# First two pairs multiplied as they come, an eighth bank for two blocks, fourth products last, and other planner assumptions in a two-layer encoder kernel

## The chip, the cores and the metric

The kernel runs on one core of one Trainium2 chip. The metric is the device time of one execution in microseconds (us), the median of three runs. Before the change it is 2682.38 us (2681.67 to 2683.91).

## The reference

Two layers of an encoder on 256 tokens of width 4096, in float32. The two large products of a layer, with `w_in` (4096 x 11264) and `w_out` (4096 x 4096), are nearly all the arithmetic.

```python
for l in range(DEPTH):                                  # DEPTH = 2
    h = rmsnorm(x, norm_w[l])
    proj = h @ w_in[l]
    aq, ak, av, ag, rq, rk, rv, rg = jnp.split(proj, SPLIT_POINTS, axis=-1)
    ...
    a_out = (jax.nn.silu(ag) * gqa_attention(aq, ak, av)).astype(x.dtype)
    ...
    r_out = (jax.nn.silu(rg.astype(jnp.float32)) * r).astype(x.dtype)
    x = x + jnp.concatenate([a_out, r_out], axis=-1) @ w_out[l]
return rmsnorm(x, final_norm)
```

## The kernel before, in words

**Blocks and pairs.** The output columns of the large products are cut into 30 blocks of 1024 columns: per layer 11 of `w_in` (`BLOCKS`) and 4 of `w_out`. The 4096 rows that are summed over are cut into 16 pairs of 256. `block()` (L1225) runs through the pairs and adds up 128x512 products in banks of the accumulator memory, named M1 to M7 (the profile calls all of them M). A scheme that saves multiplications is used: each of the five pairs in `SEVEN` (0, 3, 6, 9, 12) takes 7 products, each of the other eleven 8. In the latter, two of the eight products use a difference of two quarters of the activations, a third array `x3` (profile: `x`), beside `x8h` and `x8l`.

**Parts.** A float32 number is kept as a high part and a low part that TensorE multiplies in one pass each. `product()` (L849) issues three matmuls for one product: high x high (L851), low weights x high (L852), high weights x low (L853). So a block has (5 x 7 + 11 x 8) x 3 = 369 matmuls. Weights come by SyncE's queue into `wraw` (5 buffers), ScalarE casts them to `whi`, VectorE subtracts to get `wlo` (rings of 5 pages). For a pair of `SEVEN`, VectorE first forms sums of weights, `wsum`. For five pairs (`FAR_PAIRS`) the second page's low part comes otherwise: ScalarE writes -`fhi` to `flo`, and a DMA on GpSimd's queue adds the weights to it from memory (L476). The activations are split in the same way by `split_pair()` (L516): a tile `full`, scaled by the norm's gains (`nw`), becomes `x8h`, `x8l`, `x3` or `x7h`, `x7l` by way of the sums `xf`.

**The order of the work** is written by a planner that runs when the program is built. It keeps an assumed clock of TensorE (`now.t`) and of VectorE and ScalarE (`Clock`), with costs such as `vector_cost` and `STEP_V`. After every product `tick()` (L771) asks `Weights.room()` whether one more step of other work (splits in `waiting`, steps of attention and retention in `tasks` and `lanes`) fits without making the weights late by these assumptions, and if so writes that step. At most `AT_ONCE` tasks are begun at a time. When a pair's operand is needed and not there, `need()` (L626) writes all the steps that it lacks at that place. Nothing of this runs on the chip: there, each engine goes through its fixed list and waits on semaphores.

**The two ends.** At the start (L1497 and on) 36 matmuls on zeros are issued (`warm()`), then the first rows of x and of weights are loaded, and pair 1 and pair 0 are split before their products. At the end, `last_combine()` (L1382) adds the last banks and the residual, squares, forms the norm for row half 0 after M3 and for row half 1 after M4, scales eight pieces of each half (`finish()`) and stores each by a DMA on SyncE's queue (L1438). In the last block the products of pair 15, and one product of pair 14 in M4, stand behind all others; M4's three are the very last.

Of the kernel before, what the change touches and what calls it, by code (L numbers as in the profile page):

```python
# [41 lines left out]
STEP_V, STEP_S = 1.0, 1.3  # L42
# [5 lines left out]
STORE, FETCH = 8.0, 12.0  # L48
FAR_LANDING = 11.0
MARGIN = 0.0  # L50
# [7 lines left out]
AT_ONCE = 2  # L58
# [4 lines left out]

SEVEN = (0, 3, 6, 9, 12)

# [67 lines left out]
]  # L133
EIGHTS = [_p for _p in range(NP) if _p not in SEVEN]
# [4 lines left out]
def pages_of(group, first=False):  # L139

    one = [(group[0], _k) for _k in (PAGE_A, PAGE_T, PAGE_B, PAGE_U)]
    rest = [(_p, _k) for _p in group[1:] for _k in (PAGE_A, PAGE_B)]
    order = []
    if first:
        order += rest[:2]
        rest = rest[2:]
    for _i, _v in enumerate(one):
        order += [_v] + rest[_i : _i + 1]
    return order + rest[len(one) :]
# [7 lines left out]
def slots_of(group, first=False):  # L157

    for _p, _k in pages_of(group, first):
        if _p in SEVEN:  # L160
            yield [(_b, _p, (ALL, _a), _k, _h) for _b, _a, _pg, _h in SEVEN_PRODUCTS if _pg == _k]
        else:
            yield [(_b, _p, (_i, _a), _k, _h) for _b, _i, _a, _pg, _h in EIGHT_PRODUCTS if _pg == _k]
# [5 lines left out]
BANKS = ("M1", "M2", "M3", "M4", "M5", "M6", "M7")  # L169
# [35 lines left out]
def vector_cost(name, n, kwargs):  # L205
    one = name in ("tensor_copy", "tensor_scalar", "tensor_scalar_mul", "tensor_scalar_add", "memset")
    return 0.15 + n * (0.00052 if one else 0.00104)


def scalar_cost(name, n, kwargs):  # L210
    return 0.2 + n * 0.00083 + (0.2 if kwargs.get("accum_out") is not None else 0.0)
# [3 lines left out]
def hybrid_encoder(  # L215
# [137 lines left out]
    class Weights:  # L353


        def __init__(self):
            self.pages = []
            for l in range(DEPTH):
                for w, n in ((w_in, N_IN), (w_out, N_OUT2)):
                    for b in range(n):  # L360
                        for g in GROUPS:
                            start = (l, b) == (0, 0) and w is w_in
                            for slot in slots_of(g, start and g is GROUPS[0]):
                                one = Page()
                                one.pair, one.kind, one.uses = slot[0][1], slot[0][3], len(slot)
                                one.far = is_far(g, one.pair, one.kind) and not (start and g in GROUPS[:2])
                                one.src, one.begun, one.low_at, one.next = [], False, None, []
                                if one.kind == PAGE_A:
                                    one.src.append(w[l, b, one.pair, 0])
                                if one.kind == (PAGE_A if one.pair in SEVEN else PAGE_B):  # L370
                                    one.src.append(w[l, b, one.pair, 1])
                                self.pages.append(one)
            near = [g for g in self.pages if not g.far]
# [12 lines left out]
        def load(self):  # L386
            if self.loaded < len(self.todo):
# [3 lines left out]
                step = 1 if self.loaded == 1 else 2  # L391
                for k in range(0, 2, step):
                    nc.sync.dma_start(r[:, k : k + step, :], src[:, k : k + step, :])
                self.raw.append(r)

# [4 lines left out]

        def parts(self, g, src, halves=(ALL,), then=None):

            g.hi = t(wp, [P, 2, NB], "whi", RING, F32R)
            g.lo = t(wp, [P, 2, NB], "wlo", RING, F32R)
            for h in halves:
                ac.copy(g.hi[:, h, :], src[:, h, :])
            g.high_at = ac.until + PASS

            def low():
                ve.after(g.high_at)  # L410
                for h in halves:
                    ve.tensor_sub(g.lo[:, h, :], src[:, h, :], f32(g.hi)[:, h, :])
# [6 lines left out]
        def far_parts(self, g, src):  # L419

            g.hi = t(wp, [P, 2, NB], "fhi", FAR, F32R)
            g.lo = t(wp, [P, 2, NB], "flo", FAR, F32R)
            ac.copy(g.hi, src)
            ac.activation(g.lo, f32(g.hi), AF.Copy, scale=-1.0)
            g.high_at, g.low_at = ac.until, ac.until + FAR_LANDING
            self.adds.append((ac.until, partial(nc.gpsimd.dma_start, g.lo, g.src[0], accum_op=ALU.add)))
            self.load()

        def begin(self, g):
# [4 lines left out]
            elif g.pair not in SEVEN:  # L434
                halves = (slice(0, 1), slice(1, 2)) if g is self.order[0] else (ALL,)
                self.parts(g, self.taken(), halves, self.load)
# [13 lines left out]
            elif g.kind == PAGE_B:  # L450
                self.parts(g, self.b, (slice(1, 2),), self.load)
# [46 lines left out]

    weights = Weights()
# [16 lines left out]
    def split_pair(p, v, whole, stage):  # L516

        gains = gains_of(p, stage)
        now_first = stage == 0 and p == 1
# [5 lines left out]
        if gains and not now_first:  # L525
            for i in range(2):
                u = v[:, :, i].rearrange("p m a t -> p (a m) t") if whole is None else whole[:, i]
                ac.activation(u, u, AF.Copy, scale=gains[i])
            yield
# [25 lines left out]
        else:  # L555
# [4 lines left out]
            if now_first:  # L560
                for i in range(2):
                    ac.activation(hi[:, i], whole[:, i], AF.Copy, scale=gains[i])
                yield
                for i in range(2):
                    ve.scalar_tensor_tensor(
                        lo[:, i], whole[:, i], gains[i], f32(hi)[:, i], op0=ALU.mult, op1=ALU.subtract
                    )
                yield
                ve.tensor_sub(x0, x0, x1)
                for i in range(2):  # L570
                    ac.activation(g4[0][:, i], x0[:, i], AF.Copy, scale=gains[i])
                yield
                for i in range(2):
                    ve.scalar_tensor_tensor(
                        g4[1][:, i], x0[:, i], gains[i], f32(g4[0])[:, i], op0=ALU.mult, op1=ALU.subtract
                    )
            else:
                if whole is None:
                    u = [w.rearrange("p i (m a t) -> p i m a t", m=MT, t=BLK) for w in (hi, lo)]
                    pieces = [(u[0][:, i], u[1][:, i], v[:, :, i]) for i in range(2)]  # L580
                else:
                    pieces = [(hi, lo, whole)]
                for h, _, src in pieces:
                    ac.copy(h, src)
                yield
                for h, w, src in pieces:
                    ve.tensor_sub(w, src, f32(h))
# [10 lines left out]
        yield  # L598

# [171 lines left out]
    def tick():  # L771
# [5 lines left out]
        while True:  # L777
# [3 lines left out]
            for v in waiting[:SPLITS] + (lanes + running() if room else []):  # L781
# [5 lines left out]
            waiting[:] = [v for v in waiting if not v.done]  # L787
            clear()
# [436 lines left out]
    def block(after_pair, phase, then, first_order=False, order=LAST_ORDER, last=None):  # L1225
# [7 lines left out]
        for g in GROUPS:  # L1233
            for slot in slots_of(g, first_order and g is GROUPS[0]):
                flat += slot
        if first_order:

            flat[:4] = sorted(flat[:4], key=lambda v: (v[4], v[2][1] == 2))

        used = list(dict.fromkeys((v[1], v[3]) for v in flat if not is_far(None, v[1], v[3])))[-RING:]  # L1240
# [7 lines left out]
        first = {b: next(i for i, v in enumerate(flat) if v[0] == b) for b in BANKS}  # L1248
        final = {b: max(i for i, v in enumerate(flat) if v[0] == b) for b in BANKS}
        left = {}  # L1250
# [5 lines left out]
        for n, (bank, p, index, k, h) in enumerate(flat):  # L1256
            tight[0] = n < 3 or n >= len(flat) - 7
            if p in firsts:
                firsts.remove(p)
                need(p, phase)  # L1260
                now.wait(operand_at[p])
# [4 lines left out]
            if n == first[bank]:  # L1266
                acc[bank] = t(pm, [P, NB], bank)
            if p in SEVEN:
# [7 lines left out]
            product(acc[bank], a, at((g.hi, g.lo), ALL, h), n == first[bank], n == final[bank])  # L1276
            follow()
            if n == final[bank]:
                finished.append((bank, partial(last or combine, bank, acc, c)))
                if bank == order[0] or n == len(flat) - 1:  # L1280
                    follow(True)
            g.uses -= 1
            if not g.uses:
                using.remove(g)
                for one in g.next:
# [11 lines left out]
    def combine(bank, acc, c):  # L1297
# [9 lines left out]
        elif bank == "M5":  # L1307
# [74 lines left out]
    def last_combine(res):  # L1382
# [10 lines left out]
        def last(bank, acc, c):  # L1393
# [17 lines left out]
            elif bank == "M3":  # L1411
# [61 lines left out]
    def first_rows(c):  # L1473
        full[c] = page([P, KG * SEQ], "full")
        step = KG * SEQ // (2 if c == 0 else 1)
        for k in reversed(range(0, KG * SEQ, step)):
            nc.sync.dma_start(full[c][:, k : k + step], xT[c, :, k : k + step])

# [7 lines left out]
    def made(p):  # L1486

        one = next(v for v in waiting if v.pair == p)
        while not one.done:
            one.step()  # L1490
        waiting.remove(one)

    def begun():
        weights.begin(next(g for g in weights.order if not g.begun))
        weights.low_parts(True)

    warm()  # L1497
    first_rows(0)
    weights.load()
    turn = Turn(0, first_rows)  # L1500
# [3 lines left out]
    for _ in range(2):  # L1504
        waiting[1].step()
    begun()
    made(1)
    weights.load()
    first_rows(1)
    for _ in range(RAWS - 2):  # L1510
        weights.load()
    first_rows(2)
    begun()
    made(0)
    begun()
    split_operand(1, 0)
    made(2)
    begun()
    made(3)
    begun()  # L1520


    for l, L in enumerate(layers):
        for bi, (one, _) in enumerate(BLOCKS):
# [9 lines left out]
            c = block(after, 2 * l + 1, 2 * l + 1 + (bi == N_IN - 1), start)  # L1534
# [81 lines left out]
```

## Time and profile before

| | |
|---|---|
| median of three runs | 2682.38 us |
| the profiled execution's own time | 2678.84 us |
| its span, first to last instruction | 2676.8 us |
| TensorE (PE) matmuls busy | 2620.1 us, 98% |
| VectorE (DVE) busy | 2134.8 us, 80% |
| ScalarE (ACT) busy | 1799.5 us, 67% |
| granted TensorE clock, mean | 0.991 |
| DMA, mean | 255 GB/s |

The helper that records VectorE's and ScalarE's operations has one line, L200, so these are told apart by their tiles. A profile row names the engine, the line, the operation, out<-in and the count. "PEq", "SPq" and the like are the engines' issuing queues. Idle time of an engine that nobody waits for costs nothing.

### The profile page before, as it was taken

Reading aid. Unit: us, or ns where it says so; the run is one execution under the profiler, and the core shown is the slowest. Engines: PE = TensorE matmul, PEld = TensorE weight load, DVE = VectorE, ACT = ScalarE, POOL = GpSimd, SP = SyncE. Lnnn points to the kernel's source line nnn. Section 1 sums busy time; section 2 is a strip of 40 time slices with the busy share of each in tenths; the row PEclk is TensorE's granted clock in tenths of the full one; section 3 lists DMA queues with packets and bytes.
Section 4 is the critical chain, followed back from the end, with each engine's and each line's share of the span. In section 5 each row is a group of like instructions: output and inputs, shape, how many; then the busy total and the mean of one; then the engine's idle time right before and its main releaser. Section 6 shows DMA issues by size and latency. Waiting matters only on the chain.

```text
span 2676.8 us, 33938 instructions
## 1 busy us (share of the span) xinstructions
PE 2620.1 (98%) x11778; PEld 2169.8 (81%) x11778; DVE 2134.8 (80%) x2620; ACT 1799.5 (67%) x2554; POOL 366.2 (14%) x508
## 2 busy tenths in 40 slices
PE   8999999999999999999999999999999999999997
PEld 6877888888888878888787888887888888788886
DVE  7787878879868888777887878877887688886775
ACT  7766776766665678655876666775676567786554
POOL 0011211211111010111111111211210111010000
PEclk8999999999999999999999999999999999999999
DMA  7888889888778777988887888887887787778886
GB/s 252 284 259 283 251 265 290 281 255 275 229 235 252 239 239 221 287 278 254 284 257 229 271 278 275 264 273 241 266 255 222 238 261 238 226 235 263 252 268 192
DMA packets 200828, 683.90 MB, mean 255 GB/s; under 512 B 24144, under 2 KB 30800, under 8 KB 200656
## 3 DMA queue, kind: packets, MB, share of 16 engines
q1 hardware_dynamic: 147760, 521.27, 55.8%
q0 software_dynamic: 52896, 160.46, 25.9%
q8 instruction: 92, 1.51, 0.2%
q14 instruction: 80, 0.66, 0.1%
HBM read 637.60 MB, written 44.04 MB: 255 GB/s over the span
## 4 chain that ended last, share of the span: by engine, by line
PE 82%; DVE 8%; DMA 6%; ACT 2%; issue 2%; POOL 1%; SPq 0%; DVEq 0%; ACTq 0%; POOLq 0%
PE M L852 26%; PE M L853 26%; PE M L851 26%; DVE wlo L200 4%; DMA wraw<-in_w_in 3%; DMA flo<-in_w_in 2%; DVE wsum L200 1%; PE ps L852 1%; PE ps L853 1%; PE ps L851 1%; DMA wraw<-in_w_out 1%; ACT whi L200 1%; DVE cb L200 0%; DVE ca L200 0%; DMA flo<-in_w_out 0%
## 5 line engine op out<-in xcount | busy, mean ns | idle before, releaser
L200 DVE TENSOR_TENSOR wlo<-wraw,whi 128x1024 fp32r<-128x1024 f32 (+1 forms) x813 | 895.5, 1119 | 305.3 <-ACT whi L200 300.4
L200 ACT CAST whi<-wraw 128x1024 fp32r<-128x1024 f32 (+1 forms) x813 | 779.7, 969 | 509.0 <-PE M L853 365.6
L851 PE MATMUL M<-whi,x8h 128*128 128x512 f32 x1536 | 600.8, 391 | 1.1 <-ACT whi L200 0.6
L852 PE MATMUL M<-wlo,x8h 128*128 128x512 f32 x1536 | 600.2, 391 | 1.2 <-DVE wlo L200 1.2
L853 PE MATMUL M<-whi,x8l 128*128 128x512 f32 x1536 | 599.1, 390 | 0.0
L851 PE MATMUL M<-whi,x7h 128*128 128x512 f32 x1050 | 410.1, 391 | 6.8 <-DVE cb L200 6.8
L852 PE MATMUL M<-wlo,x7h 128*128 128x512 f32 x1050 | 409.5, 390 | 1.7 <-DVE wlo L200 1.7
L853 PE MATMUL M<-whi,x7l 128*128 128x512 f32 x1050 | 409.1, 390 | 0.0
L200 DVE TENSOR_TENSOR wlo<-wsum,whi 128x1024 fp32r<-128x1024 f32 x300 | 365.3, 1218 | 25.9 <-ACT whi L200 25.7
L200 ACT CAST whi<-wsum 128x1024 fp32r<-128x1024 f32 x300 | 314.8, 1049 | 97.8 <-PE M L853 92.5
L851 PEld LDWEIGHTS M<-whi,x8h 128*128 128x128 f32 x1536 | 289.9, 189 | 61.8 <-ACT whi L200 1.7
L852 PEld LDWEIGHTS M<-wlo,x8h 128*128 128x128 f32 x1536 | 289.9, 189 | 61.2 <-DVE wlo L200 2.2
L853 PEld LDWEIGHTS M<-whi,x8l 128*128 128x128 f32 x1536 | 289.7, 189 | 60.6
L200 ACT CAST fhi<-wraw 128x1024 fp32r<-128x1024 f32 x148 | 155.7, 1052 | 199.2 <-PE M L853 191.8
L476 POOL DMA_DIRECT2D flo<-in_w_in x108 | 97.1, 899 | 1100.2 <-ACT flo L200 1008.0
L851 PEld LDWEIGHTS M<-whi,x7h 128*128 128x128 f32 x1050 | 197.6, 188 | 49.3 <-DVE cb L200 8.4
L852 PEld LDWEIGHTS M<-wlo,x7h 128*128 128x128 f32 x1050 | 197.6, 188 | 42.3 <-DVE wlo L200 2.3
L853 PEld LDWEIGHTS M<-whi,x7l 128*128 128x128 f32 x1050 | 197.5, 188 | 41.1
L200 DVE TENSOR_TENSOR wsum<-wraw 128x1024 f32<-128x1024 f32 x150 | 182.8, 1219 | 48.2 <-DMA wraw<-in_w_in 37.1
L851 PE MATMUL M<-whi,x 128*128 128x512 f32 x512 | 200.9, 392 | 11.8 <-ACT x L200 10.8
L852 PE MATMUL M<-wlo,x 128*128 128x512 f32 x512 | 200.9, 392 | 1.9 <-DVE wlo L200 1.9
L853 PE MATMUL M<-whi,x 128*128 128x512 f32 x512 | 201.0, 393 | 0.7 <-DVE x L200 0.7
(223 smaller groups left out, 3401.5 us busy)
## 6 DMA issues: line engine op xcount, KB each, us to landing
wraw<-in_w_in SPq DMA_DIRECT2D x703, 512.0 KB, 5.0
wraw<-in_w_out SPq DMA_DIRECT2D x256, 512.0 KB, 4.8
flo<-in_w_in POOLq DMA_DIRECT2D x108, 512.0 KB, 7.8
flo<-in_w_out POOLq DMA_DIRECT2D x40, 512.0 KB, 7.4
full<-next_dram POOLq DMA_DIRECT2D x18, 512.0 KB, 8.4
p_dram<-room POOLq DMA_DIRECT2D x64, 128.0 KB, 4.9
pT<-p_dram POOLq DMA_DIRECT2D x16, 512.0 KB, 8.7
next_dram<-room POOLq DMA_DIRECT2D x40, 128.0 KB, 5.4
```

The costliest lines, as they stand in the source:

```text
L200: return call(out, *args, **kwargs)
L476: self.adds.pop(0)[1]()
L851: nc.tensor.matmul(out, a[0], b[0], start=start, stop=False)
L852: nc.tensor.matmul(out, a[0], b[1], start=False, stop=False)
L853: nc.tensor.matmul(out, a[1], b[0], start=False, stop=stop)
```

## The change

It has five parts.

1. **Pairs 1 and 0 of the first block are multiplied as they come** (`NATIVE`). Their weights are loaded into `fhi`, `flo` and `wsum` buffers that stand empty at that time (`load_whole`), their activations are only scaled, and one float32 matmul (L1379) stands for each product in place of three. Pair 0 takes 8 products there, as the third array isn't formed. Both pairs are still split afterwards, for the blocks that follow.
2. **In the first two blocks an eighth bank stands in for the third array** (`PLAIN`, `PLAIN_PRODUCTS`). M8 uses the bank `ps` that attention and retention use later. `x3` is formed afterwards from the parts (`third()`), a step at a time, before the third block.
3. **In the last block the M4 products of five pairs** (`DELAYED`) stand behind all others: 10 products, 30 matmuls, in place of 3 products, 9 matmuls. The weights that they need are written to rooms of activations that are no longer used (`dead_room`), so those pages are split in halves.
4. **The last scalings are dealt out otherwise**: all eight pieces of row half 0 directly behind its norm.
5. **Other planner assumptions**: `STEP_V`, `S_FIXED`, `MARGIN`, `AT_ONCE`.

```diff
-STEP_V, STEP_S = 1.0, 1.3
+STEP_V = 1.6
+STEP_S = 1.3
+V_FIXED = 0.15
+S_FIXED = 0.12
-MARGIN = 0.0
+MARGIN = 0.2
-AT_ONCE = 2
+AT_ONCE = 3
+DELAYED = (10, 11, 13, 14, 15)
+NATIVE = (1, 0)
+WHOLE = 4
+PLAIN = 2
...
+PLAIN_PRODUCTS = [
+    ("M3", 1, 0, PAGE_A, 1),
+    ("M8", 1, 1, PAGE_A, 1),
...
+        def load_whole(self, n):
+            g = self.wholes[n]
+            tag, bufs, dt = (("fhi", FAR, F32R), ("flo", FAR, F32R), ("wsum", 2, F32), ("wsum", 2, F32))[n]
+            g.raw = f32(t(wp, [P, 2, NB], tag, bufs, dt))
+            for k in (1, 0) if n == 0 else (ALL,):
+                nc.sync.dma_start(g.raw[:, k, :], g.src[0][:, k, :])
+            g.begun, g.high_at, g.low_at = True, 0.0, 0.0
...
+    def third(p, hi, lo, g, one):
+        while held[0] + pledged() >= PAGES:
+            yield
+        one.at_work = True
+        v = page([P, 2, 2, P], "x3f")
+        d, e = v[:, 0], v[:, 1]
+        for u, v in ((d, hi), (e, lo)):
+            ve.tensor_sub(u, f32(v)[:, :, :P], f32(v)[:, :, P:])
+        ve.tensor_add(d, d, e)
+        yield
+        ac.copy(g[:, 0], d)
+        yield
+        ve.tensor_sub(g[:, 1], d, f32(g)[:, 0])
...
-            return v[1] == NP - 1 or (last and v[0] == order[-1] and v[1] == NP - 2 and (v[1], v[3]) in used)
+            return v[1] == NP - 1 or last and v[0] == order[-1] and v[1] in DELAYED
...
+                if first_order and p in NATIVE:
+                    while p not in as_it_comes:
+                        next(v for v in waiting if v.pair == p).step()
+                    now.wait(as_it_comes[p][1])
+                else:
+                    need(p, phase)
+                    while not plain and any(v.pair == p for v in thirds):
+                        third_step()
...
+            if g.whole:
+                nc.tensor.matmul(acc[name], a, g.raw[:, h, :], start=n == first[name], stop=n == final[name])
+                now.t += WHOLE * MM[NB]
+            else:
+                product(acc[name], a, (g.hi[h], g.lo[h]), n == first[name], n == final[name])
...
+        elif bank == "M8":
+            ve.tensor_add(cb[:, 1, :], cb[:, 1, :], acc["M8"])
+            free_bank()
...
                 r[0] = last_rstd(0)
-                for n in (0, 2):
-                    finish(0, n, ac)
+                for n, e in ((0, ac), (1, ve), (2, ac), (3, ve), (5, ve), (4, ac), (6, ve), (7, ve)):
+                    finish(0, n, e)
             elif bank == "M4":
                 combine(bank, acc, c)
                 square(1, c, 0)
-                finish(0, 7, ve)
                 r[1] = last_rstd(1)
-                for n, e in ((1, ve), (6, ve), (3, ve), (4, ac), (5, ve)):
-                    finish(0, n, e)
...
     warm()
     first_rows(0)
+    weights.load_whole(1)
+    first_rows(1)
     weights.load()
+    for n in range(2, 2 * len(NATIVE)):
+        weights.load_whole(n)
+        weights.load()
...
-            c = block(after, 2 * l + 1, 2 * l + 1 + (bi == N_IN - 1), start)
+            c = block(after, 2 * l + 1, 2 * l + 1 + (bi == N_IN - 1), start, plain=l == 0 and bi < PLAIN)
```

How the instructions move is shown at three places, before and after, in the order in which they stand on one engine.

TensorE, the first products of the program, right behind the 36 matmuls on zeros. Before (`whi`, `wlo` are parts of weights, `x8h`, `x8l` parts of pair 1's activations, the numbered M are banks):

```order
L851 MATMUL M_248<-whi,x8h 128x512
L852 MATMUL M_248<-wlo,x8h 128x512
L853 MATMUL M_248<-whi,x8l 128x512
L851 MATMUL M_258<-whi,x8h 128x512
L852 MATMUL M_258<-wlo,x8h 128x512
L853 MATMUL M_258<-whi,x8l 128x512
```

Now (`fhi`, `flo`, `wsum` hold whole weights here, `full` is the scaled x):

```order
L1379 MATMUL M_195<-fhi,full 128x512
L1379 MATMUL ps<-fhi,full 128x512
L1379 MATMUL M_207<-fhi,full 128x512
L1379 MATMUL M_209<-fhi,full 128x512
L1379 MATMUL M_207<-flo,full 128x512
L1379 MATMUL ps<-flo,full 128x512
L1379 MATMUL M_195<-flo,full 128x512
L1379 MATMUL M_209<-flo,full 128x512
L1379 MATMUL M_195<-wsum,full 128x512
```

Sixteen such matmuls have taken the place of 45, and nothing of ScalarE's casts or VectorE's subtractions of weights stands ahead of them: in all PE has 29 fewer.

ScalarE, in the first block of the second layer, where the last two pairs' activations (from `cb`, the end of the first layer) are scaled and cast. Before:

```order
L200 COPY ca<-M_11784 128x512
L200 CAST whi<-wraw 128x1024
L200 CAST whi<-wsum 128x1024
L200 CAST whi<-wraw 128x1024 x3
L200 ACTIVATE cb<-cb,nw 128x8x32 x4
L200 CAST x8h<-cb 128x256 x4
L200 CAST x_12422<-cb 128x256
```

Now:

```order
L230 CAST whi<-wraw 128x1024
L230 CAST whi<-wraw 128x512
L230 ACTIVATE cb<-cb,nw 128x8x32 x4
L230 CAST x8h<-cb 128x256 x4
L230 CAST fhi<-wraw 128x1024
L230 ACTIVATE flo<-fhi 128x1024
L230 CAST x_12314<-cb 128x256
L230 COPY ca<-M_11761 128x512
```

The scaling and the casts of `x8h` have moved ahead of the bank's copy to `ca`, of a far page (`fhi`, `flo`) and of five casts of weights that stood ahead of them.

ScalarE, in the sixth block of the second layer, where a far page is made and the queries `q` of the next attention group are cast. Before:

```order
L200 CAST fhi_16073<-wraw_15947 128x1024
L200 ACTIVATE flo_16074<-fhi_16073 128x1024
L200 CAST whi_16090<-wraw_16002 128x1024
L200 CAST whi_16109<-wsum_16008 128x1024
L200 CAST whi_16120<-wraw_16011 128x1024
L200 CAST whi_16137<-wraw_16045 128x1024
L200 CAST whi_16148<-wsum_16118 128x1024
L200 CAST whi_16167<-wraw_16077 128x1024
L200 CAST whi_16179<-wraw_16033 128x512
L200 CAST aqh_16185<-q_16085 128x4x128 x2
```

Now:

```order
L230 CAST fhi_16053<-wraw_15948 128x1024
L230 ACTIVATE flo_16054<-fhi_16053 128x1024
L230 CAST aqh_16059<-q_15960 128x4x128 x2
L230 CAST whi_16069<-wraw_16002 128x1024
L230 CAST whi_16090<-wsum_15999 128x1024
```

The queries' cast stands directly behind the far page in place of seven casts later; on GpSimd's queue the load of `q` is still the row ahead of that page's DMA.

More of the change, by code (lines that the diff above doesn't have):

```diff
@@ L434, in begin @@
             elif g.pair not in SEVEN:
-                halves = (slice(0, 1), slice(1, 2)) if g is self.order[0] else (ALL,)
-                self.parts(g, self.taken(), halves, self.load)
+                self.parts(g, self.taken(), then=self.load)
             elif g.kind == PAGE_A:
@@ L497, in room, with dead_room @@
             )
+    rooms = []
+    def dead_room():
+        if not rooms:
+            two = [("x3", NP - len(SEVEN), [P, 2, 2, P], "p k s t -> p (k s t)")] * 2
+            two += [(v, NP - len(SEVEN), [P, 2, SEQ], "p k s -> p (k s)") for v in ("x8h", "x8l")]
+            one = [(v, len(SEVEN), [P, 7, P], "p k t -> p (k t)") for v in ("x7l", "x7h")]
+            for n in range(16):
+                rooms.extend(two)
+                rooms.extend(one if n % 2 else ())
+        tag, bufs, shape, flat = rooms.pop(0)
+        return t(ap, shape, tag, bufs, F32R).rearrange(flat)[:, :NB]
     weights = Weights()
@@ L528, in split_pair @@
                 ac.activation(u, u, AF.Copy, scale=gains[i])
+            if stage == 0 and p in NATIVE:
+                as_it_comes[p] = (whole, ac.until + PASS)
             yield
@@ L780, in tick @@
                 return
-            for v in waiting[:SPLITS] + (lanes + running() if room else []):
+            for v in waiting[:SPLITS] + (lanes + running() + (thirds[:1] if not waiting and not (turning and turning[0].first) else []) if room else []):
                 if v.ready <= now.t:
@@ L787, in tick @@
             waiting[:] = [v for v in waiting if not v.done]
+            thirds[:] = [v for v in thirds if not v.done]
             clear()
@@ L1503, in hybrid_encoder @@
     split_operand(0, 0)
[L1504 to L1515, printed above, removed]
+    for p in NATIVE:
+        made(p, False)
+    for p in NATIVE:
+        made(p)
     split_operand(1, 0)
[L1517 to L1520, printed above, removed]
+    waiting.sort(key=lambda v: v.pair in NATIVE)
+    for _ in range(START):
+        begun()
     for l, L in enumerate(layers):
```

217 lines of the change are left out of this document (132 added, 85 removed).

## The prediction

> **What bounds the kernel now.** I read the page's head first, then the busy time by stage, to find where TensorE (PE) stands still, and then the rows of the stages where it does. The head:
>
> ```profile
> span 2676.8 us, 33938 instructions
> PE 2620.1 (98%) x11778; PEld 2169.8 (81%) x11778; DVE 2134.8 (80%) x2620; ACT 1799.5 (67%) x2554; POOL 366.2 (14%) x508
> ```
>
> PE is the bound: busy for all but 57 us. So an edit is worth what it takes from PE's work or from those gaps. The stages, PE alone (length, busy time and matmuls, granted clock, DMA share, GB/s):
>
> ```profile
> core 0: us, PE busy (x), PEclk, DMA share, GB/s
> 0.00:44.67 44.67, 32.12 (x120) 0.85 0.74 257
> 111.60:330.00 218.40, 213.10 (x951) 1.00 0.87 269
> 980.00:1000.00 20.00, 15.83 (x66) 0.93 0.68 207
> 1290.00:1310.00 20.00, 17.61 (x71) 0.91 0.87 294
> 1410.00:1425.00 15.00, 10.01 (x34) 0.77 0.55 170
> 1425.00:1840.00 415.00, 414.88 (x1896) 1.00 0.86 268
> 1840.00:1862.00 22.00, 15.54 (x63) 0.84 0.73 254
> 2300.00:2330.00 30.00, 26.33 (x114) 0.94 0.75 217
> ```
>
> From 1425 to 1840 us PE never waits. The time is lost at the two ends and in a few gaps, each followed by some microseconds at a lower clock. The start, PE's rows, then ScalarE's (ACT) first two on data:
>
> ```profile
> 1.09 5.42 PE L1484 MATMUL ps<-junk 128*128 128x256 bf16 x36 [1.09 <-DVE junk L200]
> 20.59 0.55 PE L851 MATMUL M<-whi,x 128*128 128x512 f32 x1 [1.01 <-ACT whi L200]
> 23.29 0.63 PE L852 MATMUL M<-wlo,x8h 128*128 128x512 f32 x1
> 23.72 0.63 PE L853 MATMUL M<-whi,x8l 128*128 128x512 f32 x1
> 51.09 0.39 PE L851 MATMUL M<-whi,x8h 128*128 128x512 f32 x1
> 57.89 0.39 PE L851 MATMUL M<-whi,x7h 128*128 128x512 f32 x1
> ```
>
> ```profile
> 4.32 0.91 ACT L200 ACTIVATE x8h<-full,nw 128x256 fp32r<-128x256 f32 x2 [2.07 <-DMA full<-in_xT]
> 6.49 0.62 ACT L200 CAST whi<-wraw 128x512 fp32r<-128x512 f32 x1 [1.26 <-DMA wraw<-in_w_in]
> ```
>
> From 51.09 to 57.89 lie 30 matmuls, so one takes 0.2267 us of PE. By 44.67 us, 120 - 36 = 84 real ones have run, worth 84 x 0.2267 = 19.0 us: 25.6 us are lost. VectorE (DVE) sets that pace (columns PE, PEld, DVE, ACT, POOL, then clock and DMA):
>
> ```profile
> core 0: us, PE busy (x) PEld busy (x) DVE busy (x) ACT busy (x) POOL busy (x), PEclk, DMA share, GB/s
> 0.00:20.00 20.00, 14.63 (x66) 9.33 (x66) 10.44 (x21) 10.61 (x20) 0.20 (x4) 1.00 0.72 265
> 20.00:45.00 25.00, 17.82 (x55) 13.16 (x56) 23.08 (x37) 21.73 (x38) 1.01 (x1) 0.73 0.76 253
> ```
>
> In 20 to 45 us DVE is busy for 23.1 of 25: PE waits for parts that DVE and ACT can't make faster.
>
> **The start.** Three rows price the pieces: the weight load of one matmul, a DVE step on a page of weights (whole and half pages mixed), and one on a quarter of a pair's activations.
>
> ```profile
> L851 PEld LDWEIGHTS M<-whi,x8h 128*128 128x128 f32 x1536 | 289.9, 189 | 61.8 <-ACT whi L200 1.7
> L200 DVE TENSOR_TENSOR wlo<-wraw,whi 128x1024 fp32r<-128x1024 f32 (+1 forms) x813 | 895.5, 1119 | 305.3 <-ACT whi L200 300.4
> L200 DVE TENSOR_TENSOR x<-full,x 128x256 fp32r<-128x256 f32 x34 | 13.8, 414 | 3.7 <-ACT x L200 3.7
> ```
>
> The change puts 16 whole float32 matmuls in the place of 45. The trace has none of that kind. At least one should cost what the three parts cost together, 3 x 0.2267 = 0.68 us; at most four passes with no weight load hidden, 4 x (0.2267 + 0.189) = 1.66. I take 0.907, four passes of 0.2267, as the change's own planner counts (`WHOLE`), near the row with loads hidden: 16 x 0.907 = 14.5 us. The Trainium skill (FP8 and Floating Point Precision, TensorE Precision Notes) says that true float32 makes four passes through the array; by that the sum is as taken, an estimate that no run here shows yet.
>
> The first needs a scaled quarter of x (4.32 + 0.91 = 5.2 us) and 256 KB of weights, which came by 6.49 us and now stand one place earlier in SyncE's queue; the zeros end at 6.5. So PE begins at 6.6 us and runs to 21.1. Meanwhile DVE gets ahead: of the 33.5 us that it works in the first 45 it loses the weights of pairs 0 and 1, some 8 steps x 1.12 = 9 us, and over the block the third arrays, 2 steps x 0.41 x 11 pairs = 9 us. Those come back as four steps a pair, 18 us, spread over the first two blocks, where DVE's idle fifth (80% busy over the span) covers them; they are due only in the third block, and uncovered they would cost up to 18. The eighth bank costs two more DVE additions and no PE time. To get as far as 84 matmuls had come, 39 of the three-part kind (8.8 us) follow. For waits left in the first block I take 2.5 us, between 0 (DVE stays ahead) and 8 (it is as late as in 20 to 45 us again). 6.6 + 14.5 + 8.8 + 2.5 = 32.4, against 44.67: **-12.2 us** (-18 to +6 by the bounds).
>
> **The middle.** Two gaps have their cause in the order, and the order has changed there. At the second layer's first block:
>
> ```profile
> 1415.10 1.70 ACT L200 ACTIVATE cb<-cb,nw 128x256 f32<-128x256 f32 x4
> 1416.70 1.31 ACT L200 CAST x8h<-cb 128x256 fp32r<-128x256 f32 x4
> 1418.83 0.80 PE L851 MATMUL M<-whi,x 128*128 128x512 f32 x1 [4.99 <-ACT x L200]
> ```
>
> The last two pairs' split was written only when PE needed it, behind five casts of weights; 34 matmuls (7.7 us) ran in that stage of 15, so 7.3 us are lost. Now it stands ahead of those casts: I take 1 us as left, **-6.3**. The second, in the second layer's sixth block:
>
> ```profile
> 1836.68 0.55 POOL L814 DMA_DIRECT2D q<-q_dram  x1
> 1837.20 0.94 POOL L476 DMA_DIRECT2D flo<-in_w_in  x1
> 1853.11 0.80 PE L852 MATMUL M<-flo,x8h 128*128 128x512 f32 x1 [6.46 <-DMA flo<-in_w_in]
> ```
>
> The far page's DMA was issued right behind the loads of `kv` and `q`, and landed 15.9 us later. The stage lost 22 - 63 x 0.2267 = 7.7 us. In the new order `q` is cast directly behind `flo`, so the loads must have been planned for an earlier time: I take 0.7 as left, **-7.0**. If `q` is not there, ACT stands still behind that cast, with `whi` casts queued behind it, and the gap stays.
>
> The other gaps (5.3 us in 111 to 330, 5.0 in 980 to 1000, 3.9 in 1290 to 1310, 3.7 in 2300 to 2330) I leave as they are: what DVE and ACT have to do there is the same. `AT_ONCE`, `STEP_V` and `MARGIN` move nearly every step, so I add one new wait of the size of 1290 to 1310's, 20 - 71 x 0.2267 = **+4** (-18, if all the others go, to +17, if as much comes as I let go).
>
> **The end.**
>
> ```profile
> 2659.42 0.69 DVE L200 TENSOR_TENSOR cb<-cb,M 128x512 f32<-128x512 f32 x1 [0.67 <-PE M L853]
> 2661.46 0.69 DVE L200 TENSOR_TENSOR ca<-ca,M 128x512 f32<-128x512 f32 x1 [0.15 <-PE M L853]
> ```
>
> ```profile
> 2662.00 1.33 ACT L200 ACTIVATE ca<-ca,last 128x512 f32<-128x512 f32 x2 [1.07 <-POOL last L347]
> 2663.24 0.58 ACT L200 ACTIVATE ps<-ca 128x512 f32<-128x512 f32 x1
> 2665.17 1.95 ACT L200 ACTIVATE ca<-ca,last 128x512 f32<-128x512 f32 x3 [0.61 <-POOL last L347]
> ```
>
> ```profile
> 2662.74 0.95 SPq L1438 DMA_DIRECT2D out<-ca  x2
> 2672.11 0.59 SPq L1438 DMA_DIRECT2D out<-cb  x1
> ```
>
> Sixteen stores leave SyncE between 2662.74 and 2672.70, 0.62 us each. Row half 0's norm is ready 2.6 us after M3's addition (2659.42 to 2662.00). PE ends at 2661.4, where M4's addition begins. M3 now ends 30 matmuls, 6.8 us, ahead of that, so half 0's eight stores run from -3.5 to +1.5 us of that end, beneath M4's matmuls. Half 1's last square waited 1.1 us (2662.15 to 2663.24) behind two scalings of half 0; that goes, so its norm is there at 2664.1 in place of 2665.17, its first store 0.7 later and eight stores after 5.0: 2669.8 against 2672.70, **-2.9 us**. The halved pages make ACT and DVE's list longer by some ten half steps (0.62 us for ACT's at 6.49); ACT's idle third hides them, and uncovered they would cost 6 us.
>
> **The sum.** 2678.84 (the profiled execution, span 2676.8 and 2.0 around it) - 12.2 - 6.3 - 7.0 + 4 - 2.9 = 2654.4. The median of the runs was 3.5 us above the profiled one: 2657.9, so 2658.
>
> **Rivals.**
> - *The planner's part gives nothing.* The two gaps move to other places. For it: nearly all steps move, by assumed costs. Against it: the stages at 1410 and 1840 lose time to an order that is gone. Start and end alone: 2682.4 - 12.2 - 2.9 = 2667. Chance 0.23.
> - *The whole matmuls run at double price,* because PE waits for their weights and the clock falls. At 20.59 PE had waited 1.01 us, and behind that a matmul takes 0.43 us (23.29 to 23.72) in place of 0.2267. 16 x 0.907 more: 2672. Chance 0.10. The Trainium skill (TensorE: Matmul & The Clock Gate, What's actually happening) lets the clock fall after an idle window of about 3.4 us; the wait at 20.59 was shorter, so here the trace is the stricter.
> - *Slower: far pages come late at eight places.* In eight blocks the new order has the far page's DMA behind four `p_dram` stores on GpSimd's queue (L809), which wait for DVE's `room`.
>
> ```profile
> 1583.57 2.23 POOL L809 DMA_DIRECT2D p_dram<-room  x4 [15.60 <-DVE room L200]
> flo<-in_w_in POOLq DMA_DIRECT2D x108, 512.0 KB, 7.8
> ```
>
>  With 3.9 us lost at each, as in 1290 to 1310, it adds 31 us: 2689. It decides once the stores hold the DMA so long that less than its 7.8 us is left before PE needs the page. Against it: at 1583.57 such stores stood ahead of a far page, and PE waited nowhere from 1425 to 1840. Chance 0.07.
> - *More gaps go than I counted:* all four that I left, and no new one: 2658 - 17.9 - 4 = 2636. Chance 0.10.
>
> That the whole matmuls aren't there is excluded by PE's order, which has 29 fewer instructions.
>
> **How the numbers follow.** Forecast 0.50, rivals as given. 0.2% (5.4 us) is about what a measurement of this kernel can tell from no change: faster means below 2677. The forecast, the first two rivals and the last are there, less a little for their spread: 0.87; same 0.06; slower 0.07. The range takes in both nearer rivals and half of the way to the last: 2640 to 2673.
>
> **What would show it.** The first L1379 matmul at 6.6 us and sixteen in 14.5 us; clock 1.0 up to 45 us and the first block's end 12 us earlier; no wait for `x` near 1400 us nor for `flo` near 1835; eight stores before PE's end plus 2 us, and 12.5 us from PE's end to the last landing. It is wrong if the whole matmuls take over 1.4 us, or if PE's waits between 45 and 2640 us come to 45 us or more.

## The result and the profile after

The changed kernel takes 2642.38 us, median of four runs (2637.64 to 2644.54), against 2683.14 (2681.67 to 2684.54, four runs of the kernel before beside them): ratio 0.9846, 95% interval 0.9829 to 0.9863. That is 40.8 us less, where the forecast of 2658 made it 25; the time is inside the range.

The head of the page after:

```profile
span 2641.8 us, 33949 instructions
PE 2611.1 (99%) x11765; PEld 2162.7 (82%) x11765; DVE 2134.4 (81%) x2640; ACT 1794.0 (68%) x2559; POOL 365.7 (14%) x510
```

VectorE (DVE) and ScalarE (ACT) do as much as before. What went are waits of TensorE (PE). The largest, first before, then after (what was waited for, us in all, times, longest):

```profile
PE M L852 <- DMA flo<-in_w_in: 12.4, 6, 6.5
PE M L851 <- ACT x L200: 10.8, 3, 5.5
PE M L851 <- DVE cb L200: 6.8, 3, 3.3
```

```profile
PE M L945 <- DVE cb L230: 10.1, 4, 3.4
PE M L946 <- DMA flo<-in_w_out: 2.5, 3, 1.1
PE M L946 <- DVE wlo L230: 2.3, 2, 1.7
PE M L946 <- DMA flo<-in_w_in: 2.0, 4, 0.9
```

The waits for `x` are gone and those for `flo` and `wlo` are small; those for `cb`, an addition that frees a bank, have grown. PE's start:

```profile
1.09 6.32 PE L1598 MATMUL ps<-junk 128*128 128x256 bf16 x36 [1.09 <-DVE junk L230]
7.25 1.02 PE L1379 MATMUL M<-fhi,full 128*128 128x512 f32 x2
8.11 1.02 PE L1379 MATMUL ps<-fhi,full 128*128 128x512 f32 x2
19.27 1.88 PE L1379 MATMUL M<-wsum,full 128*128 128x512 f32 x4
20.58 0.79 PE L945 MATMUL M<-whi,x8h 128*128 128x512 f32 x1
```

A whole matmul shows as two records; from 7.25 to 8.11 runs one, so it takes 0.86 us, and sixteen take 13.7, without a wait. No wait of PE follows until 87 us.

The accounting below takes, in each trace, the time from one matmul's start to the next, less 0.2267 us (0.118 for one of 256 columns, 0.859 for a whole one), and adds up what is left over by blocks of 1024 columns, block 0 first. A block is counted from its second product on, so the wait for bank M3, which comes ahead of that product, stands with the block before. It is the time that PE loses, slow clock included; the four runs that tell most are beside the two kernels.

| us lost in blocks | before | after | e1 | e5 | e9 | e11 |
|---|---|---|---|---|---|---|
| 0 | 20.2 | 4.0 | 2.9 | 3.7 | 3.0 | 3.3 |
| 1 to 3 | 6.9 | 8.6 | 9.8 | 6.8 | 7.0 | 6.3 |
| 10, 11 | 7.1 | 4.4 | 13.5 | 6.2 | 4.7 | 4.0 |
| 14 | 4.4 | 3.1 | 6.2 | 7.2 | 1.8 | 3.6 |
| 15 (second layer's first) | 8.6 | 2.9 | 8.3 | 9.2 | 1.9 | 2.1 |
| 20 | 9.3 | 0.2 | 4.5 | 8.8 | 0.7 | 0.7 |
| 25, 26 | 6.5 | 3.2 | 13.6 | 5.4 | 3.9 | 3.2 |
| all | 65.6 | 30.5 | 63.4 | 54.3 | 27.0 | 25.5 |

The tail of the changed kernel: the additions of M3 and of M4 on DVE, the latter at PE's end, then the first and the last store of each row half on SyncE.

```profile
2623.23 0.69 DVE L230 TENSOR_TENSOR cb<-cb,M 128x512 f32<-128x512 f32 x1 [0.67 <-PE M L947]
2630.03 0.69 DVE L230 TENSOR_TENSOR ca<-ca,M 128x512 f32<-128x512 f32 x1 [1.61 <-PE M L947]
```

```profile
2626.56 0.34 SPq L1550 DMA_DIRECT2D out<-ca  x1
2630.42 0.60 SPq L1550 DMA_DIRECT2D out<-cb  x1
2633.33 0.33 SPq L1550 DMA_DIRECT2D out<-ca  x1
2637.21 0.57 SPq L1550 DMA_DIRECT2D out<-cb  x1
```

Half 0's stores run from -3.5 to +1.0 us of PE's end, and the span ends 11.8 us behind that end, against 15.3 (2661.46 to 2676.8) before.

### The profile page after: what moved, and what is told of

The parts are those of the page before. It is cut to its first block, busy times and chain, and to the rows that moved or that the text cites. A ratio compares the mean times of both kernels' runs of the same rounds, so it can differ in the third digit from the quotient of the medians.

```text
span 2641.8 us, 33949 instructions
## 1 busy us (share of the span) xinstructions
PE 2611.1 (99%) x11765; PEld 2162.7 (82%) x11765; DVE 2134.4 (81%) x2640; ACT 1794.0 (68%) x2559; POOL 365.7 (14%) x510
## 4 chain that ended last, share of the span: by engine, by line
PE 85%; DMA 5%; DVE 4%; ACT 3%; issue 2%; POOL 0%; SPq 0%; DVEq 0%; POOLq 0%; ACTq 0%
PE M L946 27%; PE M L945 27%; PE M L947 27%; DVE wlo L230 2%; DMA flo<-in_w_out 1%; DMA wraw<-in_w_in 1%; PE ps L946 1%; PE ps L947 1%; PE ps L945 1%; DMA wraw<-in_w_out 1%; DMA flo<-in_w_in 1%; ACT whi L230 1%; ACT ca L230 1%; DVE wsum L230 1%; DVE cb L230 0%
## 5 line engine op out<-in xcount | busy, mean ns | idle before, releaser
L945 PE MATMUL M<-whi,x8h 128*128 128x512 f32 x1514 | 591.8, 391 | 0.9 <-DVE ca L230 0.9
L946 PE MATMUL M<-wlo,x8h 128*128 128x512 f32 x1514 | 591.1, 390 | 0.0
L947 PE MATMUL M<-whi,x8l 128*128 128x512 f32 x1514 | 590.6, 390 | 0.0
L230 ACT CAST fhi<-wraw 128x1024 fp32r<-128x1024 f32 (+1 forms) x148 | 154.7, 1046 | 175.3 <-PE M L947 172.7
L945 PEld LDWEIGHTS M<-whi,x7h 128*128 128x128 f32 x1043 | 196.0, 188 | 51.4 <-DVE cb L230 11.8
L947 PEld LDWEIGHTS M<-whi,x7l 128*128 128x128 f32 x1043 | 196.0, 188 | 40.8
L946 PE MATMUL M<-wlo,x 128*128 128x512 f32 x476 | 186.3, 391 | 2.3 <-DVE wlo L230 2.3
L945 PE MATMUL M<-whi,x 128*128 128x512 f32 x476 | 185.9, 391 | 0.0
L947 PE MATMUL M<-whi,x 128*128 128x512 f32 x476 | 185.9, 391 | 0.0
```

What stands on the lines that cost most here:

```text
L230: return call(out, *args, **kwargs)
L945: nc.tensor.matmul(out, a[0], b[0], start=start, stop=False)
L946: nc.tensor.matmul(out, a[0], b[1], start=False, stop=False)
L947: nc.tensor.matmul(out, a[1], b[0], start=False, stop=stop)
```

## The experiments

Twelve kernels. The question was first which part had made the unexpected share of the gain, then whether that part follows a rule.

**e1, one constant put back.**

```diff
-S_FIXED = 0.12
+S_FIXED = 0.2
```

> The changed kernel with one constant put back: S_FIXED 0.2 in place of 0.12. Theory A: this constant alone makes the middle's gain (35.0 us of span, less 12.6 at the start and 3.6 behind PE's end: 18.9), because the two waits belong to the order that it sets. Then the waits for x near 1406 us (5 us) and for flo near 1843 us (6.5 us) are back, the start and the end stay as in the changed kernel, and the time is 2642.4 + 19 = 2661 (2655 to 2667). Theory B: the waits went because the first blocks were written anew and everything behind them shifted. Then the time stays at 2642 (2637 to 2648) and neither wait is there. Theory C, several constants together: half of it, about 2652.

Measured 2682.5 us (2675.6 to 2685.0), ratio to before 1.0005 (0.9993 to 1.0018): with this one constant the whole gain of the change is gone, though block 0 still loses 17 us less. More came back than any of the theories had: besides the two old waits (the one for `flo` in block 20 now 2.4 us in place of 6.5) there were two that neither kernel had, in blocks 11 and 26. One of them, on PE, and the split on ScalarE that it waited for:

```profile
1064.89 0.50 PE L945 MATMUL M<-whi,x 128*128 128x512 f32 x1 [0.80 <-ACT x L230]
1070.04 0.80 PE L947 MATMUL M<-whi,x 128*128 128x512 f32 x1 [4.42 <-DVE x L230]
```

```profile
1057.75 1.29 ACT L230 ACTIVATE ca<-ca,nw 128x256 f32<-128x256 f32 x3
1066.28 0.41 ACT L230 CAST x<-ca 128x256 fp32r<-128x256 f32 x1 [0.49 <-DVE ca L230]
```

It is the kind of block 15 before: the last pairs' split stands too late. From the scaling of the activations (1057.75) to the cast of their third array (1066.28) there are 8.5 us.

**e2, the constant alone in the kernel before.**

```diff
-    return 0.2 + n * 0.00083 + (0.2 if ...)
+    return 0.12 + n * 0.00083 + (0.2 if ...)
```

> The kernel before with one constant changed: S_FIXED 0.12 in place of 0.2, nothing else. Theory A (this constant makes the middle's gain): no wait for x near 1434 us, none for flo near 1853 us, start and end as before; 2683.1 - 19 = 2664 (2656 to 2670). Theory B (the rewritten first blocks did it): 2683 within 4 us, and waits of 5 us and more somewhere in the middle.

2664.8 (2661.9 to 2671.1), ratio 0.9949 (0.9930 to 0.9969): as theory A had it. PE loses 49.5 us in place of 65.6; block 15 loses 1.7 and block 20 0.2. A new wait for `flo` of 2.9 us came in block 4, where 6.0 us are lost.

**e5, all four assumptions put back** (`STEP_V` 1.0, `S_FIXED` 0.2, `MARGIN` 0, `AT_ONCE` 2).

> The changed kernel with all four assumptions put back (STEP_V 1.0, S_FIXED 0.2, MARGIN 0, AT_ONCE 2), so the start, the eighth bank and the end alone. S_FIXED alone put back gave 2682.5, with two waits of 5.4 us for x at 1065 and 2393 us that neither kernel had. Theory A: these two come from S_FIXED 0.2 together with STEP_V 1.6 or AT_ONCE 3, that is from assumptions that don't fit each other, and go with the old set; the waits near 1419 us (5 us) and 1848 us stay: 2682.5 - 15 = 2667 (2660 to 2673), the prediction's rival without the planner's part. Rival: the old set gives waits of the same sum at other places, 2682.

2665.7 (2658.0 to 2670.4), ratio 0.9947 (0.9927 to 0.9968). The two waits of e1 are gone; the old ones are back. ScalarE in block 15, and what PE waited there:

```profile
1395.33 1.65 ACT L230 COPY cb<-room 32x256 f32<-32x256 f32 x4
1399.52 1.05 ACT L230 CAST whi<-wraw 128x1024 fp32r<-128x1024 f32 x1
1400.47 1.05 ACT L230 CAST whi<-wsum 128x1024 fp32r<-128x1024 f32 x1
1405.89 1.70 ACT L230 ACTIVATE cb<-cb,nw 128x256 f32<-128x256 f32 x4
```

```profile
1410.19 0.79 PE L945 MATMUL M<-whi,x 128*128 128x512 f32 x1 [5.55 <-ACT x L230]
```

A cast lasts 1.05 us, but the next starts 0.95 us behind it. The planner counts 0.2 + 1024 x 0.00083 = 1.05 with the old constant and 0.97 with the new one. The split needs the activations in `cb`, which come by four sets of four copies (`COPY cb<-room`), and the planner writes a set only when its own ScalarE is nearly done with the one ahead. With the higher cost all this is written later: the last set stands 62.5 us behind the block's start (1332.8) here and 55.6 behind it (1326.7) in the changed kernel. The same rows there:

```profile
1382.29 1.65 ACT L230 COPY cb<-room 32x256 f32<-32x256 f32 x4
1389.33 1.70 ACT L230 ACTIVATE cb<-cb,nw 128x256 f32<-128x256 f32 x4
1390.93 1.31 ACT L230 CAST x8h<-cb 128x256 fp32r<-128x256 f32 x4
```

The split does not follow the copies at once. The planner begins it only when some pair of the block is finished (`turn_over()`), or when PE is to use it (`need()`). In the changed kernel it comes 62.6 us behind the block's start, and PE waits nowhere for it; in e5 it comes at 73.1. The planner's own clock, printed as it writes the two kernels, says why: in e5 the last set is done 0.7 us behind the end of pair 11, and no other pair ends before the need; in the changed kernel it is done 7.5 us ahead of the end of pair 9. Its test `room()` holds the split back in neither: it finds room after every product in between.

So the new constant does not win by being true. It fits the casts of weights, but a set of copies takes 1.65 us in both kernels, as the old constant counts it (4 x (0.2 + 256 x 0.00083)), and the new one counts 1.33. What it does is to bring the copies ahead of an earlier end of a pair.

**e9, only `S_FIXED` new**, the other three old.

> The changed kernel with the other three assumptions put back (STEP_V 1.0, MARGIN 0, AT_ONCE 2), S_FIXED left at 0.12: the fourth corner of a square whose others are 2642.4 (all new), 2682.5 (S_FIXED alone old) and 2665.7 (all old). Theory A: S_FIXED decides nearly all, the other three move little (180 of 11787 rows on TensorE stand elsewhere), so 2642 to 2648. Theory B: the other three are worth 17 us here too, one way or the other, because each order is a draw: 2652 or more.

2641.4 (2640.0 to 2645.8), ratio 0.9859 (0.9844 to 0.9873). The square is complete:

| us | other three old | other three new |
|---|---|---|
| `S_FIXED` 0.2 | 2665.7 (e5) | 2682.5 (e1) |
| `S_FIXED` 0.12 | 2641.4 (e9) | 2642.4 (changed) |

With 0.12 the other three do nothing that can be measured; with 0.2 they cost 17. The planner's part of the change is `S_FIXED`, worth 24 us (ratios to before 0.9947 and 0.9859; the kernel before took 2681 to 2683 us beside each corner).

**e6 and e7, `S_FIXED` 0.09 and 0.15.**

> The changed kernel with S_FIXED 0.09 in place of 0.12. In the trace casts of 128x1024 that follow each other start 0.95 to 0.96 us apart; 0.12 + 1024 x 0.00083 = 0.97, with 0.09 it is 0.94. Theory A (what counts is that the planner's ScalarE isn't late by its own clock): 0.09 is as near as 0.12, no wait above 3 us comes, 2642 within 5. Theory B (0.12 is one lucky order among many): waits of 4 us and more come at new places, 2650 to 2670.

> The changed kernel with S_FIXED 0.15: a cast of 128x1024 counts 1.0 us, 0.04 more than the 0.96 between two starts in the trace, half of the error that 0.2 makes. Theory A (the error decides): between 2642 and 2682, near 2655, as the order has some splits later. Theory B (each order is a lottery): anywhere from 2642 to 2682, with no relation to the error; below 2647 or above 2670 speaks for it.

2654.9 (2654.2 to 2656.3) and 2656.0 (2653.7 to 2658.5). Neither theory holds alone. With 0.09 no wait is longer than 2.2 us, but there are eight for `flo` from `w_in` (10.9 us in all); with 0.15 the split in block 15 is late again (waits of 1.2 and 3.1 us), beside 10.6 us for such `flo`. The split begins 62.2 us behind the block's start with 0.09, 62.6 with 0.12, 66.4 with 0.15 and 73.1 with 0.2, and PE waits 0, 0, 4.3 and 5.6 us for it (the last in e5): by steps, since it can begin only at the end of a pair, and not in proportion to the error. The waits for `flo`, some 10 us, fall as the order happens to be. Whether 0.12 is best because it is nearest to the casts' spacing or by its draw of short waits stays open.

**e8, the same correction for VectorE.**

```diff
-V_FIXED = 0.15
+V_FIXED = 0.07
```

> The changed kernel with V_FIXED 0.07 in place of 0.15. VectorE's subtractions of 128x1024 that follow each other start 1.14 us apart in the trace; the planner counts 0.15 + 1024 x 0.00104 = 1.215, with 0.07 it is 1.135. If costs that fit the trace are what helps, this does for VectorE what S_FIXED 0.12 did for ScalarE: of the 26 us still lost between the products some 5 to 10 go, 2633 to 2638. Rival: VectorE's surplus of 0.08 us was a reserve for waits that the planner doesn't see; without it parts come late, 2648 or more.

2661.3 (2658.3 to 2664.2), ratio 0.9931 (0.9904 to 0.9957): 19 us slower than the changed kernel, in the rival's range. Its longest waits:

```profile
PE M L946 <- DMA flo<-in_w_in: 8.4, 6, 2.8
PE M L946 <- DMA flo<-in_w_out: 6.3, 3, 3.0
PE M L946 <- DVE wlo L230: 4.6, 6, 1.0
```

The rival's reason holds only in part: the waits for `wlo`, which DVE makes, come to 4.6 us, and those for `flo`, which ACT and a DMA make, to 14.7. A cost that fits the spacing in the trace is not better by that alone.

**e3, one whole pair only** (`NATIVE = (1,)`).

> The changed kernel with NATIVE = (1,): only pair 1 is multiplied whole, eight matmuls of 0.86 us; pair 0 is split and multiplied by 7 products of three parts. Theory A: the whole matmuls pay because VectorE and ScalarE get 13.7 us ahead while they run; with half of that PE waits for parts of pair 0 or 2 behind the eighth whole matmul, at 14.1 us, for 4 to 8 us in all, less 2.1 us of work saved (8 x 0.86 = 6.9 against 21 x 0.2267 = 4.8): 2645 to 2649. Rival: pair 1 alone covers the parts (VectorE was not the limit of the start): the 2.1 us are won, 2640.

2653.4 (2651.7 to 2653.9), 11 us slower than the changed kernel, more than theory A had. Block 0 loses 12.6 us in place of 4.0:

```profile
15.32 0.50 PE L945 MATMUL M<-whi,x7h 128*128 128x512 f32 x1 [0.83 <-ACT x7h L230]
51.00 0.80 PE L947 MATMUL M<-whi,x7l 128*128 128x512 f32 x1 [3.97 <-DVE x7l L230]
```

The first four waits are the expected ones, at pair 0. The longest comes at 51 us for another pair's split; that DVE still lacks then what it lacked at 15 us fits this, but was not tested. Of the 11 us, 6.7 are there by block 1 (105.8 against 99.1); blocks 3 to 6 lose 9.7 more than in the changed kernel, in small waits, and blocks 1 and 2 lose 5.9 less.

**e4, the eighth bank in one block** (`PLAIN = 1`).

> The changed kernel with PLAIN = 1: the eighth bank stands in for the third array in the first block only. Theory A: the wait of 3.4 us for cb at 187.4 us comes from the second block's eighth bank; it goes, but the third arrays of eleven pairs (four VectorE steps of 0.41 us each, 18 us) must be made in the first block or as the second needs them, where VectorE has 10 to 17 us free: PE waits 3 to 8 us for x in the second block. Sum between -0.5 and +5: 2642 to 2647. Rival: VectorE covers the third arrays, and only the wait for cb goes: 2639.

2644.8 (2643.1 to 2645.1). The wait for `cb` at 187.4 went, and block 1 got one for `flo` and one for a third array instead:

```profile
131.67 0.50 PE L946 MATMUL M<-flo,x8h 128*128 128x512 f32 x1 [2.72 <-DMA flo<-in_w_in]
185.70 0.80 PE L947 MATMUL M<-whi,x 128*128 128x512 f32 x1 [3.87 <-DVE x L230]
```

**e11, M3's products ahead of M8's.**

```diff
-PLAIN_ORDER = ("M8", "M3", "M4", "M2")
+PLAIN_ORDER = ("M3", "M8", "M4", "M2")
```

> The changed kernel with the last products of the first two blocks in the order M3, M8, M4, M2 in place of M8, M3, M4, M2. TensorE waits 2.6 us at 99.1 and 3.4 us at 187.4 for the addition that frees M3; in VectorE's list M8's addition (0.60 us to the next start) stands ahead of M3's, and now behind it. Theory A: VectorE is behind there, so each wait becomes 0.6 us shorter, no more, and the time 1.2 us less, 2641. Theory B: the wait hangs on the order of the banks alone; with M3's last product six matmuls earlier both waits nearly go, 2637.

DVE's additions in the changed kernel, and the matmul that waits for M3's (the second `cb<-cb` below):

```profile
97.42 0.42 DVE L230 TENSOR_TENSOR x<-x3f,x 128x256 fp32r<-128x256 f32 x1
97.75 0.68 DVE L230 TENSOR_TENSOR cb<-cb,ps 128x512 f32<-128x512 f32 x1
98.35 0.68 DVE L230 TENSOR_TENSOR cb<-cb,M 128x512 f32<-128x512 f32 x1
```

```profile
99.08 0.50 PE L945 MATMUL M<-whi,x7h 128*128 128x512 f32 x1 [2.60 <-DVE cb L230]
```

In e11 they are

```profile
98.28 0.50 PE L945 MATMUL M<-whi,x7h 128*128 128x512 f32 x1 [2.04 <-DVE cb L230]
185.99 0.50 PE L945 MATMUL M<-whi,x7h 128*128 128x512 f32 x1 [0.62 <-DVE cb L230]
190.12 0.50 PE L945 MATMUL M<-whi,x8h 128*128 128x512 f32 x1 [0.76 <-DVE ca L230]
```

The first wait shrank by 0.6 us, as theory A says: weights and a step of a third array stand ahead of the additions, and DVE is behind. The second fell from 3.4 to 0.6, with a new one of 0.8 behind it, but the order made only 0.6 us of that too: PE had lost 2.6 us to a far page at 129.5, where the changed kernel loses 0.5, and so came later to the same addition. The time is 2639.6 (2636.7 to 2641.4); against 2642.4 (2637.6 to 2644.5) this is not told apart.

**e10, two pairs delayed in place of five** (`DELAYED = (14, 15)`).

> The changed kernel with DELAYED = (14, 15): M4 of two pairs, four products, 12 matmuls (2.7 us), stands behind M3's end instead of 30 (6.8 us). In the changed kernel the first store of row half 0 leaves 3.3 us behind M3's addition, and eight stores take 4.5 us; half 1 is ready 3.3 us behind TensorE's end, and the span ends 11.8 us behind it. Theory: with two pairs half 0's stores run from 0.6 to 5.1 us behind TensorE's end and half 1's wait for them until 9.5: 13.5 us from TensorE's end to the end of the span, and 1.7 us more, 2644. Rival: what helped at the end is the new dealing of the scalings, not the delayed products: 11.8 us as now, 2642.

2643.3 (2639.8 to 2645.9) is not told apart from the changed kernel either; the trace shows the end 2.9 us longer. PE's last matmul starts at 2629.02 there (2629.61 in the changed kernel), and the span ends at 2644.1. DVE tells why:

```profile
2629.31 1.28 DVE L230 TENSOR_SCALAR cb<-cb,last 128x512 f32<-128x512 f32 x3 [0.69 <-POOL last L377]
2630.50 0.75 DVE L230 SCALAR_TENSOR_TENSOR ca<-ca,last,fn 128x512 f32<-128x512 f32 x1
2631.16 0.75 DVE L230 SCALAR_TENSOR_TENSOR cb<-cb,last,fn 128x512 f32<-128x512 f32 x1
2631.82 0.68 DVE L230 TENSOR_TENSOR ca<-ca,M 128x512 f32<-128x512 f32 x1
```

Not the stores' queue is what the delay clears, as expected, but DVE: with 2.7 us between the banks M4's addition stands behind half 0's scalings. That addition begins 2.8 us behind the start of PE's last matmul in place of 0.4, which is 2.4 of the 2.9.

**e12, e9 and e11 together.**

> The changed kernel with both edits that did not cost: the last products of the first two blocks in the order M3, M8, M4, M2, and STEP_V 1.0, MARGIN 0, AT_ONCE 2 with S_FIXED 0.12. Alone they gave 2639.6 and 2641.4 against 2642.4, and 25.5 and 27.0 us lost between the matmuls against 30.5. If the two add up, 22 us are lost there: 2634 to 2636. Rival: both differ from the changed kernel only by what one run differs from the next, and the time is 2639 to 2643.

2642.2 (2641.2 to 2642.5), ratio 0.9853 (0.9832 to 0.9873): they do not add up, and no version was found that beats the changed kernel.

## Why the prediction was right, and where it was too small

- **Start: -12.2 forecast; -14.8 measured for the work that it was summed over, and -12.6 by block 1 of the table.** That -12.2 is so near to -12.6 is luck: two errors of some 2.5 us cancel. The 16 whole matmuls and 39 of the others are done at 29.9 us, where the forecast had 32.4 and the kernel before stood at 44.67. Nothing was waited for there, where 2.5 us stood. The whole matmul costs 0.86 us, taken as 0.907. By the Trainium skill (FP8 and Floating Point Precision, TensorE Precision Notes) true float32 makes four passes; at 0.2267 us each that is an estimate of 0.907, 0.05 above the trace. PE began 0.65 us late, because the zeros took 6.32 us in place of 5.42. Block 0's last matmul starts at 95.4 against 110.4, 15.0 earlier; the wait for M3's addition then gives 2.4 back (99.1 against 111.7).
- **The eighth bank "costs no PE time": this step failed.** PE waits 2.6 and 3.4 us for M3's addition behind M8's, where the kernel before waits 0.2 and nothing; by the table the first lies in block 0 and the second in block 1. e11 shows that M8's place ahead of M3's makes only 0.6 us of each: most is DVE's delay, by three steps for weights (94.95 to 97.42 us ahead of the first) and a third array's. That the third arrays are covered by DVE in the third block holds; e4 shows the price when they are due in the second.
- **The two gaps with a cause in the order: -6.3 and -7.0 forecast, -5.7 and -9.1 measured** (blocks 15 and 20). GpSimd's queue in block 20 now has `q` 13 us ahead of the far page, and another far page right behind the `p_dram` stores:

```profile
1801.89 0.56 POOL L908 DMA_DIRECT2D q<-q_dram  x1
1815.34 0.88 POOL L487 DMA_DIRECT2D flo<-in_w_in  x1 [12.89 <-ACT flo L230]
1833.64 1.66 POOL L903 DMA_DIRECT2D p_dram<-room  x3 [0.17 <-issue]
1835.28 0.97 POOL L487 DMA_DIRECT2D flo<-in_w_in  x1
```

  The slower rival rested on that last pair; PE lost 0.2 us in that block.
- **"The other gaps I leave as they are", and one new wait, +4: this step failed.** The reason given, that DVE and ACT have the same work there, is no reason: when that work is written is what the assumptions set. The gaps were also larger than the sum had them (24.9 us by the table, 17.9 in the sum). All stages beside block 0, 15 and 20 came to -4.1 us up to PE's end (+1.7 in blocks 1 to 3, -2.7 in 10 and 11, -1.3 in 14, -3.3 in 25 and 26, +1.5 elsewhere). The forecast had +4, so that is 8.1 us of the 10.6 by which the span's fall (35.0) beat the sum's (24.4); the `flo` of block 20 gave 2.1 of the rest.
- **The rivals.** That more gaps go (2636, given 0.10) is what happened in part. The whole matmuls at double price and the planner's part giving nothing did not come.
- **End: -2.9 forecast, -3.6 measured**; half 0's stores lie where they were put. e10 varied the delayed products; the new dealing of the scalings (part 4) was not run by itself.
- **The planner as a whole: -9.3 forecast** (-6.3 - 7.0 + 4), -23.3 by e5. Start and end alone were put at 2667; e5, which is just that, gave 2665.7.
- **The median.** It lay 4.3 us above the profiled execution before and 1.2 below it after, so the two profiled executions differ by 35.3 us, not 40.8, and the account above is of those 35. Single runs of before went from 2669.6 to 2688.0.

## What to carry to other kernels

Where a planner writes the order, an assumed cost is a lever as real as an instruction: one constant, 0.08 us, was worth 24 us here, and put back alone it undid the whole change. A truer cost is not a better one by that: 0.12 fits the casts and not the copies, and a correction that fits DVE's subtractions lost 19 us (e8). So treat such a constant as a number to try with its neighbours, and look in the trace for the event that the late work just missed, here the end of a pair. A forecast for such a change should not leave the other gaps as they are: give them a range of their own.

## What the hardware showed that was not expected

Below 4 us, how long PE stands still does not settle whether its clock falls. In the experiment with `S_FIXED` 0.09 a wait of 1.82 us is followed at once by matmuls 0.43 us apart, at a granted clock of 0.53 until 135; in the kernel before a wait of 3.29 us is followed by matmuls at the full pace of 0.23, at a granted clock of 1.00.

```profile
131.78 0.64 PE L946 MATMUL M<-flo,x8h 128*128 128x512 f32 x1 [1.82 <-DMA flo<-in_w_in]
132.22 0.63 PE L947 MATMUL M<-fhi,x8l 128*128 128x512 f32 x1
```

```profile
158.98 0.50 PE L852 MATMUL M<-flo,x8h 128*128 128x512 f32 x1 [3.29 <-DMA flo<-in_w_in]
159.31 0.39 PE L853 MATMUL M<-fhi,x8l 128*128 128x512 f32 x1
159.54 0.40 PE L851 MATMUL M<-fhi,x8h 128*128 128x512 f32 x1
```

In the 14 profiles there are 45 stops of 1.9 to 3.6 us (from start to start, beyond 0.2267) with no other over 0.5 us in the 10 us ahead. Of these 24 are followed by the slow pace within nine matmuls; so are all nine such stops of 4 us and more. The Trainium skill (TensorE: Matmul & The Clock Gate, What's actually happening) puts the fall behind one idle window of about 3.4 us; a stop half as long was enough here. What else decides it, these runs do not show.
